# Second mixer matrix of an encoder trunk: three of seven partial sums read out by ScalarE and added on GpSimd

## The chip, the cores and the metric

One Trainium2 chip, one of its cores. The metric is the device time of one execution in microseconds (us); lower is better. A core has TensorE (PE; its weight loads are listed apart as PEld), VectorE (DVE), ScalarE (ACT), GpSimd (POOL) and SyncE (SP), which here issues the DMAs. Each works through its own queue of instructions in the order in which they stand there, and waits on semaphores for the others.

## The reference

Two layers over 1024 tokens of width 1024, all in float32. Each layer mixes tokens with two kinds of attention and then runs a channel mixer with a hidden width of 4096:

```python
h = rmsnorm(x, g_mlp[l]) * (1.0 + scale_m[:, None]) + shift_m[:, None]
x = x + gate_m[:, None] * (jnp.square(jax.nn.relu(h @ w_ff1[l])) @ w_ff2[l])
```

The change lies in the second product of this mixer, `... @ w_ff2[l]`, and in the sum into `x`.

## The kernel before

Everything is held transposed: a tile `xT` has 128 channels on the partitions and 1024 tokens along them, and `xs` is the list of the eight such tiles of the residual `x`.

A float32 product is made from three products of rounded halves. `split` (lines 200 to 202) writes the rounded high part on ACT (a CAST, L201) and the rest on DVE (L202), and `mm3` (L208, L209, L210) multiplies high by high, high by low and low by high into one PSUM bank. The hidden activations come back from memory in the same way through `load_split` (line 1118): a DMA (L1120), a CAST on ACT (L1121) and a subtraction on DVE (L1122).

The mixer (`mixer`) computes 14 sixteenths of the hidden width with a fast block multiplication: seven products, numbered p = 1 to 7, in place of eight. The second matrix runs in steps: `steps` has 21 of them for each layer, each for one output group q (of four) and up to three blocks k of the hidden width. The four groups begin at different blocks, so that the first step has one block, the second two, and the last steps two, one, three and two; the rest have three. `ff2_step` (line 1313) does one product of one step: three matmuls for each block (L208 to L210, 128x512 columns), and then adds the PSUM bank, times the gate, to its quadrant of `x`, with one DVE instruction (L1323). Below, that is called a read-out.

Products of one step share banks, and this is what makes the read-outs urgent:

```python
ORDER = (1, 5, 6, 3, 7, 2, 4)
CHAIN = {1: "x", 6: "x", 7: "x", 4: "x", 5: "z", 3: "z", 2: "y"}
```

Products 1, 6, 7 and 4 accumulate one on top of the other in one bank `px`; 5 and 3 in a bank `pyz`; 2 has a bank of its own, also called `pyz`. Product 6 may not begin before product 1 has been read out, 7 not before 6 has, 4 not before 7 has, and 3 not before 5 has. The banks of the next step are others.

The quadrants of `x` that the products reach: 1 and 2 the same one, 6 and 3 the same one, 5 and 7 the same one, 4 one alone.

Beside the products, DVE and ACT split the weights of products five ahead (`wq`, in eight buffers, L201 and L202) and the activations `ho` (L1121 and L1122). POOL makes the sums of weights that products 5, 6, 3 and 7 need, four for each step (`weight_operands`, L1131), from raw weights `wr` that SP loads (L1177). The tiles of the first matrix's results, `u`, come from a pool of seven buffers (`unit`, line 1194); the second matrix doesn't use it.

The order of instructions in each queue isn't that of the program: a planner goes through it with a model of the costs of its own and orders each queue by the times at which instructions become ready in that model. So a product's matmuls can stand between those of another product, and the first steps of the second matrix run among the last products of the first.

Of the kernel before, what the change touches and what calls it, by code (L numbers as in the profile page):

```python
# [12 lines left out]
AF = mybir.ActivationFunctionType  # L13
ALU = mybir.AluOpType
# [23 lines left out]
def hybrid_trunk(  # L38
# [6 lines left out]
    V, A, G, T = nc.vector, nc.scalar, nc.gpsimd, nc.tensor  # L45
# [31 lines left out]
    def nm(s):  # L77
        uid[0] += 1
        return f"{s}_{uid[0]}"

    def slab(s, shape=(P, 1024), dt=F32):
        return arena.tile(list(shape), dt, tag="slab", name=nm(s))
# [7 lines left out]
    def bank(s="pb"):  # L90
        return psb.tile([P, CH], F32, tag="pb", name=nm(s))

    def cs(ch):
        return slice(ch * CH, (ch + 1) * CH)
# [35 lines left out]
    for i in range(8):  # L130
        t = slab("xrow")
# [150 lines left out]
    ps = bank("ppos")  # L282
# [51 lines left out]
    for ch in range(2):  # L334
        for k in range(8):
            ps = bank("pyT")
# [824 lines left out]
    def mixer(l, hq, gate_m):  # L1161
# [4 lines left out]
        def chain_bank(c):  # L1166
            if c == "x":
                return bank("px")
            return pool["S"].tile([P, CH], F32, tag="S", name=nm("pyz"))
# [17 lines left out]
        def product(ps, w, ops, first):  # L1187

            mm3(ps, [(w[0][:, k, :], w[1][:, k, :], t[:, 0, :], t[:, 1, :]) for k, t in enumerate(ops)], first,
                skip_group_check=True)  # L1190
# [3 lines left out]
        def unit(s):  # L1194
            return pool["ff"].tile([P, CH], F32, tag="u", name=nm(s), bufs=7)
# [117 lines left out]
        def ff2_step(n, p, w, st):  # L1313
            _, q, ks = steps[n]
            c = CHAIN[p]
            if p in FIRST:
                st[c] = chain_bank(c)
            ps = st[c]
            product(ps, w, [ho[k, p] for k in ks], p in FIRST)
            row, ch = {1: (0, 0), 6: (0, 1), 7: (1, 1), 4: (1, 0), 5: (1, 1), 3: (0, 1), 2: (0, 0)}[p]  # L1320
            nt = q + 4 * row
            x = xs[nt][:, cs(ch)]
            V.scalar_tensor_tensor(x, ps, gate_m[:, nt:nt + 1], x, op0=ALU.mult, op1=ALU.add)  # L1323
            for k in ks:
                left[k, p] = left.get((k, p), 4) - 1
                if not left[k, p]:
                    free[0] += 1
# [7 lines left out]
        for n in range(len(work) + AHEAD):  # L1335
            if n < len(work):
                kind, i, p = work[n]
                ws.append(get_w(i, p) if kind == 1 else get_w2(i, p))
            if n >= AHEAD:
                kind, i, p = work[n - AHEAD]  # L1340
                s = st.setdefault((kind, i), {})
                (ff1_step if kind == 1 else ff2_step)(i, p, ws[n - AHEAD], s)
                if kind == 1:
                    if i == 15:
                        free[0] += 8 if p == ORDER[0] else 4
                    if p == 4 and l + 1 < depth and 1 < i < 14 and i % 2:
                        ada(l + 1, (1, 0, 2, 4, 3, 5)[i // 2 - 1], slab, slab)
                fill()
# [115 lines left out]
```

## Time and profile before

| | us |
|---|---|
| median of 3 runs | 3271.41 |
| range of the runs | 3270.94 to 3275.39 |
| the profiled execution | 3277.75 |
| its span, first to last instruction | 3275.9 |
| second matrix, layer 0 | about 1338 to 1635 |
| second matrix, layer 1 | about 2938 to 3214 |

The rows further down are from the page of the profiled execution and from views of its trace. Busy times add up what the records of an engine cover; a PE record overlaps the next one, so a busy PE isn't a PE at its peak. A wait is listed with the instruction that ended last before the waiting one could start. Times in the trace count from the first instruction.

### The profile page before, as it was taken

The page shows a single profiled execution, that of the slowest core. Times are in us where ns is not written, and L with a number is a line of the kernel's source. Part 1 is how long each engine was busy: PE and PEld are TensorE (multiplying, and loading weights), DVE is VectorE, ACT ScalarE, POOL GpSimd, SP SyncE. Part 2 cuts the span into 40 slices and gives each one's busy share as a digit, 9 for nine tenths or more (in the row PEclk, how much of TensorE's full clock was granted, in tenths as well). Part 3 has the DMA queues.
Part 4 walks back from the last instruction along what each step waited for, and adds up shares of the span by engine and source line. Part 5 has one row for each costly group of instructions (what it writes and reads, how often), then busy time and mean ns, then how long its engine had stood idle before and what let it go on. Part 6 is the DMA issues. An engine that isn't in the chain of part 4 may idle for free.

```text
span 3275.9 us, 43644 instructions
## 1 busy us (share of the span) xinstructions
PE 3070.8 (94%) x15104; PEld 2461.4 (75%) x15104; DVE 2334.4 (71%) x3812; ACT 1252.1 (38%) x2436; POOL 857.5 (26%) x876
## 2 busy tenths in 40 slices
PE   6999999999996989999989999999999799999998
PEld 6878886777775767777778788777778577777777
DVE  8566667667559987888864666676763786678885
ACT  5233336553223322444332233365531333343442
POOL 5110112222232232332252101132222323223320
PEclk9999999999998999999999999999999899999999
DMA  6544334115715864644424443341244144464442
GB/s 250 161 125 109 105 93 125 45 54 178 240 65 178 263 215 154 209 145 143 116 100 115 127 113 107 90 126 36 62 138 151 48 161 145 142 212 134 146 126 93
DMA packets 357430, 437.81 MB, mean 134 GB/s; under 512 B 30492, under 2 KB 236506, under 8 KB 357210
## 3 DMA queue, kind: packets, MB, share of 16 engines
q1 hardware_dynamic: 357210, 435.03, 43.3%
q8 instruction: 119, 1.95, 0.3%
q14 instruction: 101, 0.83, 0.1%
HBM read 305.00 MB, written 112.62 MB: 127 GB/s over the span
## 4 chain that ended last, share of the span: by engine, by line
PE 68%; DVE 14%; DMA 8%; issue 4%; POOL 3%; ACT 2%; SPq 1%; DVEq 0%; ACTq 0%; POOLq 0%
PE pd L208 8%; PE pd L209 8%; PE pd L210 8%; PE smla L787 5%; PE px L208 4%; PE pom L821 4%; PE px L210 4%; PE px L209 4%; DVE wq L202 3%; DMA wada<-in_w_ada_dram 3%; PE pyz L210 3%; PE pTm L806 3%; PE pyz L208 3%; PE pyz L209 3%; DMA ho<-hid_d 2%
## 5 line engine op out<-in xcount | busy, mean ns | idle before, releaser
L208 PE MATMUL pd<-h,wh 128*128 128x512 f32 x768 | 308.5, 402 | 1.5 <-ACT wh L201 1.5
L209 PE MATMUL pd<-h,wh 128*128 128x512 f32 x768 | 301.8, 393 | 0.0
L210 PE MATMUL pd<-h,wh 128*128 128x512 f32 x768 | 301.8, 393 | 0.0
L601 POOL TENSOR_SCALAR pna<-pna,sm 128x384 f32<-128x384 f32 x128 | 81.0, 635 | 615.7 <-DVE sm L600 506.0
L794 POOL TENSOR_SCALAR pmla<-pmla,sm 128x1024 f32<-128x1024 f32 x128 | 145.3, 1135 | 339.4 <-DVE sm L793 259.1
L1131 POOL TENSOR_TENSOR s<-wr 128x512 f32<-128x512 f32 (+3 forms) x74 | 98.3, 1329 | 457.6 <-DMA wr<-in_w_ff_dram 292.9
L514 DVE RECIPROCAL gate<-gate 128x512 f32<-128x512 f32 x64 | 214.2, 3347 | 0.7
L208 PE MATMUL px<-h,wq 128*128 128x512 f32 x512 | 204.3, 403 | 10.1 <-ACT u L1205 10.0
L789 DVE TENSOR_REDUCE sm<-smla 128x1 f32<-128x1024 f32 x128 | 156.6, 1224 | 79.2 <-PE smla L787 64.4
L1122 DVE TENSOR_TENSOR ho<-ho 128x512 fp32r<-128x512 f32 x196 | 161.6, 830 | 67.0 <-ACT ho L1121 66.6
L210 PE MATMUL px<-h,wq 128*128 128x512 f32 x512 | 201.1, 395 | 6.1 <-DVE wq L202 6.1
L209 PE MATMUL px<-h,wq 128*128 128x512 f32 x512 | 202.3, 396 | 0.0
L202 DVE TENSOR_TENSOR wq<-s,wq 128x512 fp32r<-128x512 f32 (+3 forms) x296 | 193.6, 670 | 1.8 <-ACT wq L201 1.8
L208 PE MATMUL px<-ho,wq 128*128 128x512 f32 x448 | 176.0, 395 | 19.4 <-DVE xT L1323 18.0
L1121 ACT CAST ho<-ho 128x512 fp32r<-128x512 f32 x196 | 121.2, 621 | 180.0 <-DMA ho<-hid_d 173.4
L792 ACT ACTIVATE pmla<-smla,sm 128x1024 f32<-128x1024 f32 x128 | 142.9, 1117 | 117.9 <-DVE sm L790 115.0
L201 ACT CAST wq<-s 128x512 fp32r<-128x512 f32 (+3 forms) x296 | 154.5, 541 | 87.0 <-PE px L210 28.8
L210 PE MATMUL pyz<-h,wq 128*128 128x512 f32 x384 | 155.8, 406 | 32.2 <-DVE wq L202 32.2
L787 PE MATMUL smla<-st,st 128*128 128x512 f32 x512 | 171.4, 415 | 6.6 <-DMA st<-st 3.5
L202 DVE TENSOR_TENSOR wq<-wr,wq 128x512 fp32r<-128x512 f32 (+3 forms) x222 | 175.0, 806 | 0.4 <-ACT wq L201 0.4
L209 PE MATMUL px<-ho,wq 128*128 128x512 f32 x448 | 174.9, 390 | 0.0
L210 PE MATMUL px<-ho,wq 128*128 128x512 f32 x448 | 173.3, 390 | 0.0
(277 smaller groups left out, 8133.7 us busy)
## 6 DMA issues: line engine op xcount, KB each, us to landing
ho<-hid_d SPq DMA_DIRECT2D x196, 256.0 KB
wada<-in_w_ada_dram SPq DMA_DIRECT2D x96, 512.0 KB
wr<-in_w_ff_dram SPq DMA_DIRECT2D x64, 512.0 KB
w<-in_w_in_dram SPq DMA_DIRECT2D x56, 512.0 KB
hid_d<-u SPq DMA_DIRECT2D x96, 256.0 KB
wr<-in_w_ff_dram SPq DMA_DIRECT2D x64, 384.0 KB
hid_d<-t SPq DMA_DIRECT2D x84, 256.0 KB
gate_d<-gate SPq DMA_DIRECT2D x64, 256.0 KB
```

The costliest lines, as they stand in the source:

```text
L201: pin(A.copy(dst_hi, src))
L202: V.tensor_tensor(dst_lo, src, dst_hi.bitcast(F32), op=ALU.subtract)
L208: T.matmul(ps, wh, mh, start=first and i == 0, stop=False, **kw)
L209: T.matmul(ps, wh, ml, start=False, stop=False, **kw)
L210: T.matmul(ps, wl, mh, start=False, stop=i == n - 1, **kw)
L514: V.reciprocal(g, g)
L787: T.matmul(ps[:, cs(ch)], a[:, t], b[:, cs(ch)], start=i == 0, stop=i == 2)
L789: V.reduce_max(sm[:, 0:1], ps, axis=AX.X)
L792: A.activation(pt, ps, AF.Exp, bias=sm[:, 1:2], scale=MLA_SCALE, accum_out=sm[:, 2:3])
L794: G.tensor_scalar(pt, pt, sm[:, 3:4], 1.0, op0=ALU.mult, op1=ALU.mult)
L821: T.matmul(p[64 * hd:64 * hd + 64, :256], vm[kk][:, h * 64:(h + 1) * 64], pTs[pair, q2, hd][:, kk, :], start=kk == 0, stop=kk == 7)
L1122: V.tensor_tensor(t[:, 1, :], t[:, 1, :].bitcast(F32), t[:, 0, :].bitcast(F32), op=ALU.subtract)
```

## The change

For products 1, 6 and 7 the read-out is now two instructions: ACT copies the bank, times the gate, into a tile `t` from the pool of the `u` tiles, and POOL adds `t` to `x`. Products 5, 3, 2 and 4 are read out by DVE as before.

```diff
             x = xs[nt][:, cs(ch)]
-            V.scalar_tensor_tensor(x, ps, gate_m[:, nt:nt + 1], x, op0=ALU.mult, op1=ALU.add)
+            if p in (1, 6, 7):
+
+                t = unit("part")
+                A.activation(t, ps, AF.Copy, scale=gate_m[:, nt:nt + 1])
+                G.tensor_tensor(x, x, t, op=ALU.add)
+            else:
+                V.scalar_tensor_tensor(x, ps, gate_m[:, nt:nt + 1], x, op0=ALU.mult, op1=ALU.add)
```

## Rows read from the trace of the kernel before

**Rows 1.** The page: busy us (share of the span) xinstructions, and the chain.

```profile
PE 3070.8 (94%) x15104; PEld 2461.4 (75%) x15104; DVE 2334.4 (71%) x3812; ACT 1252.1 (38%) x2436; POOL 857.5 (26%) x876
PE 68%; DVE 14%; DMA 8%; issue 4%; POOL 3%; ACT 2%; SPq 1%; DVEq 0%; ACTq 0%; POOLq 0%
```

**Rows 2.** Busy time by stretch: length, PE, PEld, DVE, ACT, POOL, clock, DMA.

```profile
1338.00:1635.00 297.00, 284.64 (x1228) 229.72 (x1227) 254.19 (x405) 126.90 (x257) 92.36 (x78) 0.99 0.48 146
2938.00:3214.00 276.00, 263.93 (x1147) 214.30 (x1148) 238.78 (x372) 113.14 (x224) 84.44 (x74) 1.00 0.45 138
```

**Rows 3.** Line L1323, whole run: ns min/median/max, and who waited (us, times).

```profile
L1323 DVE SCALAR_TENSOR_TENSOR xT<-px,mod,xT x168: 732/739/753, 1341.0 to 3213.6; 128x512 f32<-128x512 f32 x168
L1323 DVE SCALAR_TENSOR_TENSOR xT<-pyz,mod,xT x126: 729/739/751, 1341.7 to 3209.7; 128x512 f32<-128x512 f32 x126
...
  PE px L208: 18.0, 15
...
  PE pyz L208: 3.5, 2
```

**Rows 4.** Instructions in order of time, 3060 to 3068: start us, us, engine, line.

```profile
3060.79 0.39 PE L208 MATMUL px<-ho,wq 128*128 128x512 f32 x1
...
3062.83 0.39 PE L208 MATMUL pyz<-ho,wq 128*128 128x512 f32 x1
...
3064.49 1.01 POOL L1131 TENSOR_TENSOR s<-wr 128x384 f32<-128x384 f32 x1 [11.39 <-DMA wr<-in_w_ff_dram]
...
3065.09 0.62 ACT L1121 CAST ho<-ho 128x512 fp32r<-128x512 f32 x1 [1.64 <-PE pyz L210]
...
3065.74 1.39 DVE L1122 TENSOR_TENSOR ho<-ho 128x512 fp32r<-128x512 f32 x1 [1.56 <-ACT ho L1121]
...
3065.77 0.39 PE L209 MATMUL px<-ho,wq 128*128 128x512 f32 x1
...
3067.06 0.74 DVE L1323 SCALAR_TENSOR_TENSOR xT<-px,mod,xT 128x512 f32<-128x512 f32 x1
...
3067.85 0.50 PE L208 MATMUL px<-ho,wq 128*128 128x512 f32 x1 [1.69 <-DVE xT L1323]
```

**Rows 5.** Groups of ACT, whole run, by shape: xcount | busy, mean ns | idle.

```profile
L1205 ACT COPY u<-px 128x512 f32<-128x512 f32 x96 | 56.0, 586 | 287.1 <-PE px L210 283.5 <-DVE u L1230 2.2 <-DVE t L1251 1.2
L1041 ACT ACTIVATE xT<-xT,mod,amlp 128x512 f32<-128x512 f32 x16 | 12.4, 807 | 10.9 <-DVE xT L1036 10.9
```

**Rows 6.** Groups of POOL, whole run, by shape.

```profile
L1131 POOL TENSOR_TENSOR s<-wr 128x512 f32<-128x512 f32 x32 | 54.0, 1686 | 108.7 <-DVE wq L202 65.7 <-DMA hid_d<-t 23.5 <-DVE xT L1036 7.3
L241 POOL TENSOR_TENSOR sums<-sums,sq 128x512 f32<-128x512 f32 x30 | 42.3, 1410 | 156.0 <-ACT sq L240 125.6 <-DVE var L248 30.0
```

**Rows 7.** Groups from 2938 to 3214, by shape.

```profile
L1122 DVE TENSOR_TENSOR ho<-ho 128x512 fp32r<-128x512 f32 x83 | 69.9, 846 | 26.7 <-ACT ho L1121 26.7
L1121 ACT CAST ho<-ho 128x512 fp32r<-128x512 f32 x79 | 49.0, 621 | 80.1 <-DMA ho<-hid_d 76.5 <-PE pyz L210 1.6 <-PE px L210 1.1
L202 DVE TENSOR_TENSOR wq<-s,wq 128x384 fp32r<-128x384 f32 x64 | 43.3, 681 | 0.0
L1131 POOL TENSOR_TENSOR s<-wr 128x384 f32<-128x384 f32 x15 | 17.1, 1138 | 132.9 <-DMA wr<-in_w_ff_dram 108.3 <-DVE wq L202 18.2 <-DVE ho L1122 6.5
```

**Rows 8.** Lines L1122 and L202 from 2930 to 3214: ns min/median/max.

```profile
L1122 DVE TENSOR_TENSOR ho<-ho x88: 672/683/1505, 2929.6 to 3168.2; 128x512 fp32r<-128x512 f32 x88
...
L202 DVE TENSOR_TENSOR wq<-s,wq x80: 279/546/1376, 2931.8 to 3200.6; 128x384 fp32r<-128x384 f32 x64, 128x256 fp32r<-128x256 f32 x12, 128x128 fp32r<-128x128 f32 x4
```

**Rows 9.** Start of the second matrix in layer 1, in order of time.

```profile
2944.45 0.68 DVE L1208 SCALAR_TENSOR_TENSOR u<-u 128x512 f32<-128x512 f32 x1
2945.15 0.34 SPq L1211 DMA_DIRECT2D hid_d<-u  x1
```

**Rows 10.** Chain that ended last, 2930 to 3216, in order of time: start us, us, what.

```profile
2999.69 5.43 DMA ho<-hid_d
...
3059.05 5.97 DMA ho<-hid_d
```

## The prediction

> **What bounds the kernel now.** The page comes first: PE is busy for 94% of the span and makes up 68% of the chain that ended last, DVE only 14% [rows 1]. So PE's matmuls set the time, and the change touches none of them. What it can win is time in which PE stands still in the second matrix, and nothing else. The busy times by stretch come next. In both stretches of the second matrix the second-busiest engine is DVE, 254 of 297 us and 239 of 276 us, some 86%, while ACT has 42% and POOL 31% [rows 2]. Hence the third view, the line of the read-outs itself and who waited for it: over the whole run PE stood still for 18.0 us, in 15 places, before a `px` matmul, and 3.5 us, in 2 places, before a `pyz` matmul, because a DVE read-out came late [rows 3]. A `px` product that waits for a read-out waits for that of product 1, 6 or 7: product 4 is the last in its bank, and the next step takes another bank. All 18.0 us therefore hang on the read-outs that are moved, and the 3.5 us on that of product 5, which stays.
>
> Last, one of these waits in order of time, to see why DVE was late [rows 4]. A product is nine matmuls from 3060.79 to 3062.83, or 2.04 us. Its read-out starts at 3067.06, four microseconds after its end, though it takes 0.74 us. In between DVE waits at the head of its queue for ACT's cast of an activation, which starts at 3065.09, and then subtracts it in 1.39 us, twice the median of 0.68 [rows 8], while POOL, whose first sum began at 3064.49, is in the middle of its sums. PE had gone on with matmuls of other products until 3065.77, and then stands still until the read-out ends: 1.69 us by the trace. So a read-out is late not because DVE has no time for it, but because it stands in a queue behind something that is itself late.
>
> **The change part by part.** There are 21 steps in each of two layers, three moved products in each: 126 read-outs, 63 for each layer.
>
> DVE loses 126 of its 294 read-outs, at 739 ns each [rows 3]: 63 x 0.739 = 46.6 us for each layer, of 239 busy in layer 1. This by itself is worth nothing, as PE and not DVE sets the time.
>
> ACT gains 63 copies out of PSUM. The nearest row is its copy of a `px` bank of the same shape into the same kind of tile, 586 ns; the dearest one of this size takes a scale and a bias from a tile, 807 ns [rows 5]. I take 0.6 us, as the bank and the tile are those of the first row: 63 x 0.6 = 38 us, from 113 to 151 busy of 276 (at 0.81 us, 164). ACT has the room. What is queued behind such a copy on ACT are the casts of weights and of activations; the weights are split five products or more ahead, so a copy that waits for its product holds up nothing that is due. Ahead of it stand casts of activations that wait for their DMA: 76.5 us of such waiting in layer 1 [rows 7]. This is the same root as DVE's lateness, one stage earlier: on DVE a read-out stands behind the wait, the cast and the subtraction, on ACT behind the wait and the cast. In the example, a copy that stood right behind the cast of 3065.09 would run from 3065.7 to 3066.3, against 3067.80 now; PE's last matmul began at 3065.77 and the next was due at 3066.0, so some 0.3 us of the wait would be left, about a fifth. Not every place is like this, since at the start of the second matrix ACT runs casts without a break and the products are short. I leave one third of the 18.0 us standing: a gain of 12.0 us. The bounds are 18.0 (nothing left) and about 2 (the copies are held up by the same DMAs for nearly as long).
>
> POOL gains 63 additions of 128x512, two inputs and an output in place. The nearest row has the same form, the running sum of squares, at 1410 ns; sums of the same shape under heavier load took up to 1686 [rows 6]. That is 63 x 1.41 = 89 us (106 at the dear end) on top of 84, or 173 to 190 of 276 us in layer 1. POOL holds that on average. Who waits for POOL now: DVE's read-out of product 3 needs the addition of product 6 into the same quadrant, and that of product 2 needs the addition of product 1. The second has four products' time; the first has one, 2.04 us, and needs 0.6 for the copy and 1.41 for the addition, so it comes just in time when POOL is free, and late by up to the four sums of a step, some 4.6 us at 1.14 each [rows 7], when it isn't. Behind product 3's read-out DVE's whole queue waits. But no product waits for the read-out of 3 itself; the next read-out of DVE that PE needs is product 5 of the next step, five products or 10 us later in a full step. So I count this as cover, not as a loss, in full steps; where it is gone is the second rival.
>
> The rest of DVE's work meets POOL more often. A subtraction of activations takes 672 ns at its shortest and 1505 at its longest [rows 8], with a mean of 846; the subtraction of a weight sum has a median of 546 [rows 8], which I take for its length when nothing disturbs it, and a mean of 681 [rows 7]. That is 83 x 0.174 + 64 x 0.135 = 23 us of stretching in layer 1, for 84 us of POOL [rows 2]: 0.27 us for each us of POOL. The 89 us of additions would then cost DVE 24 us, so of the 46.6 us it keeps 22. The read-outs from PSUM themselves don't stretch: 729 to 753 ns over all 294 [rows 3]. As the two `pyz` waits hang on DVE's lateness, I let them grow by half: a loss of 1.8 us, between 0 and, if they quadrupled, 10.
>
> The Trainium skill, SBUF — State Buffer, section "Who interferes with whom", says that VectorE and GpSimd share one pair of ports, that a VectorE instruction with two SBUF inputs contends with a GpSimd instruction that reads SBUF, and that the later one is blocked until the other ends; one with a single SBUF input isn't touched. The traces agree in kind: the read-outs, with one input in PSUM, never stretch, and the longest subtraction is about its shortest plus most of an addition. By its letter each addition could hold DVE up for its full length, in place of the third that I take; that is the third rival.
>
> The tiles of the pool of seven are new to the second matrix. Its first steps run among the last products of the first matrix, whose `u` tiles are still to be squared and stored: one square starts only at 2944.45 and its store is issued at 2945.15 [rows 9], when the second step is already under way. A copy of the second step may have to wait for that store. Bounds: nothing, or two short products, some 4 us, in each layer; I take 1 us for both layers, as the planner can bring the square forward.
>
> Sum: 12.0 - 1.8 - 1.0 = 9.2 us off the profiled execution's 3277.75, or 0.28%. The median of the runs lies 6.3 us below that execution; the same 9.2 us off the median gives 3262.2.
>
> **The rivals.** First, the lateness only changes its engine: ACT's copies stand behind the same activation loads, the waits move from DVE to ACT and 2 to 5 us are left of the gain, which the two losses eat. For it speaks that the chain runs through an activation load of over 5 us just before two of the waits of layer 1 [rows 10]; against it that ACT is idle for over half of the time and its casts keep their length (the activation cast's mean of 621 ns [rows 7] is the 0.62 us of the example [rows 4]), so that the two causes that lie on DVE, the subtraction and its stretching, fall away. Time: 3269 to 3272, no change. This includes the case that the planner orders the queues anew and what is won in one place is lost in another.
>
> Second, and on the other side: POOL's queue becomes the place where read-outs are late. Its additions stand in order among weight sums, and the first sum of a step waits for its weights, 108 us in layer 1 [rows 7], once 11.39 us [rows 4]. An addition behind it makes DVE's read-out of product 3 late by that much, and DVE then holds up the splits and the read-out of product 5. PE's cover is 10 us in a full step but only 3.4 in a step of one block and 6.8 in one of two; it decides when the addition is over 3.4 us late in the five short steps of a layer, or over 10 in a full one. If in each short step PE loses 2.5 us (about half of the four sums), that is 12.5 us for each layer and 25 in all; less the 12.0 of gain, 13 us slower: 3284. For it speaks the tight timing of product 6 and the length of POOL's waits; against it that the planner puts an addition ahead of a sum that isn't ready in its model.
>
> Third, DVE becomes the bound: each addition blocks DVE for its whole 1.41 us, so DVE has 239 - 46.6 + 89 = 281 us in 276 and the stretch grows by 5 us or more in each layer: 3281 or more. The measured third speaks against it.
>
> **How the numbers follow.** Chances: the forecast (6.5 to 20 us faster) 0.50; the first rival, within 6.5 us, 0.27; the second 0.17, the third 0.06. Predicted 3262. A measurement of this kernel can tell about 0.2%, 6.5 us, from no change. The low end, 3250, is all 21.5 us of waits for read-outs gone; the high end, 3282, takes in the first rival, the third at its mildest and the milder half of the second. The chances of faster, same and slower are 0.50, 0.27 and 0.23.
>
> **What would show it.** PE's waits for L1323 before `px` should be gone, and the waits for the new ACT line be about 6 us in all; the copy should take 0.59 to 0.61 us, the addition 1.3 to 1.5; DVE's busy share in the two stretches should fall from 86% to about 79%, POOL's rise to over 60%, and the mean subtraction of activations grow from 0.84 to over 1.0 us. If PE waits for the new copies as much as it did for DVE, the first rival holds; if DVE's read-outs wait for POOL and PE then for `pyz` or for splits, the second; if DVE's busy share rises, the third. The prediction is wrong if the planner's new order costs PE time in places that have nothing to do with the read-outs.

## The result, and the profile after

The changed kernel takes 3323.88 us at the median of four runs (3315.98 to 3324.31), beside 3271.90 for the kernel before: the ratio is 1.0155, with a 95% interval of 1.0142 to 1.0168. Forecast were 3262 us, in a range of 3250 to 3282. The profiled execution took 3323.59 us, its span is 3321.6, 45.7 us over that of before.

All of it lies in the second mixer matrix. The first view shows the busy times of its two stretches, without the first 9 us in layer 0 and the first 19 in layer 1, in the columns of [rows 2]:

```profile
1340.00:1655.00 315.00, 283.87 (x1192) 222.69 (x1190) 257.41 (x325) 154.66 (x303) 182.31 (x140) 0.99 0.43 131
2958.00:3258.00 300.00, 272.95 (x1151) 216.38 (x1150) 244.88 (x308) 146.80 (x286) 178.60 (x139) 0.98 0.42 128
```

POOL's time doubled, as forecast. DVE lost 126 of its 294 read-outs and is busy as long as before in us (245 in layer 1, where [rows 2] has 239). Its share fell to 82%, because the stretch grew. The lengths come from the starts of the last matmuls of the first and of the second matrix, here of layer 1 (count: ns min/median/max, first and last start, and the last starts are those used):

```profile
L210 PE MATMUL px<-h,wq x512: 387/389/793, 964.1 to 2956.7; 128*128 128x512 f32 x171
...
L210 PE MATMUL px<-ho,wq x448: 387/389/628, 1331.8 to 3257.9; 128*128 128x512 f32 x150
```

From 2956.7 to 3257.9 are 301.2 us; the same two starts lie 276.6 apart in the kernel before. Layer 0 gives 304.6 and 278.7. Together that is 50.5 us more. Below, such a length, of layer 1, is called the stretch.

Whom did PE wait for? Waits of the whole run (us in total, times, longest):

```profile
PE pyz L210 <- DVE wq L202: 68.1, 46, 8.4
...
PE pyz L208 <- DVE xT L1329: 15.2, 13, 5.1
...
PE px L208 <- ACT part L1326: 6.6, 8, 1.3
```

The 18.0 us before `px` [rows 3] are down to 6.6 us, now for ACT's copies. The 3.5 us before `pyz` [rows 3] are 15.2. And the wait for L202, the low halves of weights that DVE splits off, is 68.1 us; the same row of the kernel before reads 32.3, nearly all of it outside the second matrix. The row of the kernel before in the whole run, the same in its second matrix of layer 1 (2938 to 3214), and that of the change there (2940 to 3258):

```profile
PE pyz L210 <- DVE wq L202: 32.3, 23, 7.2
```

```profile
PE pyz L210 <- DVE wq L202: 0.2, 1, 0.2
```

```profile
PE pyz L210 <- DVE wq L202: 14.7, 11, 3.6
```

The three differences make 36 us. The rest lies in short gaps: between matmuls, which start 0.227 us apart when nothing holds them up, the gaps of 0.05 to 0.25 us beyond that add up to 16.3 us in the two stretches, against 5.5 in the kernel before. Most of them stand right behind a wait.

The groups of layer 1 show why DVE is late. Shape, count | busy us, mean ns | idle before, from 2958 to 3258:

```profile
L1327 POOL TENSOR_TENSOR xT<-xT,part 128x512 f32<-128x512 f32 x63 | 91.9, 1466 | 43.0 <-ACT part L1326 43.0
L1122 DVE TENSOR_TENSOR ho<-ho 128x512 fp32r<-128x512 f32 x83 | 91.4, 1105 | 34.3 <-ACT ho L1121 34.3
...
L202 DVE TENSOR_TENSOR wq<-s,wq 128x384 fp32r<-128x384 f32 x64 | 54.4, 857 | 3.7 <-ACT wq L201 3.7
...
L202 DVE TENSOR_TENSOR wq<-wr,wq 128x384 fp32r<-128x384 f32 x48 | 34.0, 714 | 0.6 <-ACT wq L201 0.6
```

Against [rows 7] the subtraction of activations went from 846 to 1105 ns, that of weight sums from 681 to 857, at the same counts: 83 x 0.259 + 64 x 0.176 = 33 us more for these two groups alone. The third group, of weights that are no sums, read in the kernel before (2938 to 3214):

```profile
L202 DVE TENSOR_TENSOR wq<-wr,wq 128x384 fp32r<-128x384 f32 x48 | 28.2, 587 | 0.0
```

A stretch in order of time shows where that lands. First DVE's queue, then the PE rows around the wait:

```profile
3137.73 0.54 DVE L202 TENSOR_TENSOR wq<-s,wq 128x384 fp32r<-128x384 f32 x1
3141.69 1.62 DVE L1122 TENSOR_TENSOR ho<-ho 128x512 fp32r<-128x512 f32 x1 [3.42 <-ACT ho L1121]
3143.23 1.38 DVE L202 TENSOR_TENSOR wq<-s,wq 128x384 fp32r<-128x384 f32 x1
3144.53 1.50 DVE L1122 TENSOR_TENSOR ho<-ho 128x512 fp32r<-128x512 f32 x1
3145.95 0.74 DVE L1329 SCALAR_TENSOR_TENSOR xT<-pyz,mod,xT 128x512 f32<-128x512 f32 x1
3146.61 0.71 DVE L202 TENSOR_TENSOR wq<-s,wq 128x384 fp32r<-128x384 f32 x1
3147.25 1.78 DVE L1122 TENSOR_TENSOR ho<-ho 128x512 fp32r<-128x512 f32 x1
3148.95 0.74 DVE L1329 SCALAR_TENSOR_TENSOR xT<-px,mod,xT 128x512 f32<-128x512 f32 x1
3149.61 0.68 DVE L1122 TENSOR_TENSOR ho<-ho 128x512 fp32r<-128x512 f32 x1
3150.21 1.61 DVE L202 TENSOR_TENSOR wq<-s,wq 128x384 fp32r<-128x384 f32 x1
3151.75 0.68 DVE L1122 TENSOR_TENSOR ho<-ho 128x512 fp32r<-128x512 f32 x1
3152.35 0.54 DVE L202 TENSOR_TENSOR wq<-wr,wq 128x384 fp32r<-128x384 f32 x1
```

```profile
3148.94 0.39 PE L209 MATMUL pyz<-ho,wq 128*128 128x512 f32 x1
3152.95 0.50 PE L210 MATMUL pyz<-ho,wq 128*128 128x512 f32 x1 [3.62 <-DVE wq L202]
```

DVE stands idle for 3.4 us until a late activation has been cast, and then has everything at once. Five of its subtractions take 1.4 to 1.8 us where an undisturbed one takes 0.54 or 0.68. The two read-outs from PSUM among them keep their 0.74. PE needs the low half of a weight that stands at the very end of the row and is still for 3.6 us. The same stretch as busy times (before, in and after the burst):

```profile
3130.00:3141.00 11.00, 11.00 (x49) 8.94 (x48) 8.27 (x12) 4.46 (x9) 5.25 (x5) 1.00 0.55 173
3141.50:3153.00 11.50, 7.88 (x36) 6.21 (x34) 11.31 (x12) 8.17 (x17) 8.63 (x7) 1.00 0.27 79
3153.00:3164.00 11.00, 11.00 (x41) 8.89 (x42) 7.88 (x10) 3.86 (x8) 5.21 (x5) 0.84 0.64 186
```

In the burst DVE is busy for 11.3 of 11.5 us, and POOL, with its own sums and the additions, for 8.6. Before and after it DVE is at 72 to 75%. The 82% of the whole stretch is a mean over these. It isn't the only such place: ahead of each of the 21 times that PE waits over 1 us for DVE in the two stretches, DVE is busy for at least 96% of the last 5 us, and for 82 to 100% of the last 10. The last row also shows what a wait costs behind its end: the granted clock is 0.84 of full in it, so for part of these 11 us TensorE ran at the lower of its two levels, 1.2 GHz and not 2.4, and 41 matmuls went through where the 11 us before the burst held 49.

### The profile page after: what moved, and what is told of

It is laid out like the page before. It is cut to its first block, busy times and chain, and to the rows that moved or that the text cites. A ratio compares the mean times of both kernels' runs of the same rounds, so it can differ in the third digit from the quotient of the medians.

```text
span 3321.6 us, 43772 instructions
## 1 busy us (share of the span) xinstructions
PE 3082.9 (93%) x15104; PEld 2458.7 (74%) x15104; DVE 2350.1 (71%) x3686; ACT 1322.7 (40%) x2562; POOL 1047.5 (32%) x1002
## 4 chain that ended last, share of the span: by engine, by line
PE 67%; DVE 16%; DMA 7%; issue 4%; POOL 3%; ACT 3%; SPq 1%; DVEq 0%; ACTq 0%; POOLq 0%
PE pd L208 8%; PE pd L209 8%; PE pd L210 8%; PE smla L787 5%; DVE wq L202 4%; PE pom L821 4%; PE px L208 4%; PE px L210 4%; PE px L209 4%; PE pyz L210 3%; PE pTm L806 3%; PE pyz L208 3%; PE pyz L209 3%; DMA wada<-in_w_ada_dram 2%; DMA ho<-hid_d 2%
## 5 line engine op out<-in xcount | busy, mean ns | idle before, releaser
L1122 DVE TENSOR_TENSOR ho<-ho 128x512 fp32r<-128x512 f32 x196 | 204.8, 1050 | 82.1 <-ACT ho L1121 82.1
L202 DVE TENSOR_TENSOR wq<-s,wq 128x512 fp32r<-128x512 f32 (+3 forms) x296 | 230.8, 798 | 8.3 <-ACT wq L201 8.3
L1327 POOL TENSOR_TENSOR xT<-xT,part 128x512 f32<-128x512 f32 x126 | 185.2, 1476 | 79.6 <-ACT part L1326 79.6
L202 DVE TENSOR_TENSOR wq<-wr,wq 128x512 fp32r<-128x512 f32 (+3 forms) x222 | 193.7, 894 | 0.7 <-ACT wq L201 0.6
L208 PE MATMUL px<-ho,wq 128*128 128x512 f32 x448 | 176.4, 395 | 6.6 <-ACT part L1326 6.6
L209 PE MATMUL px<-ho,wq 128*128 128x512 f32 x448 | 175.7, 392 | 0.0
```

Source lines behind the costliest of these rows:

```text
L202: V.tensor_tensor(dst_lo, src, dst_hi.bitcast(F32), op=ALU.subtract)
L208: T.matmul(ps, wh, mh, start=first and i == 0, stop=False, **kw)
L209: T.matmul(ps, wh, ml, start=False, stop=False, **kw)
L1122: V.tensor_tensor(t[:, 1, :], t[:, 1, :].bitcast(F32), t[:, 0, :].bitcast(F32), op=ALU.subtract)
L1327: G.tensor_tensor(x, x, t, op=ALU.add)
```

## The experiments

All times are medians beside runs of the kernel before on the same chip (3269.8 to 3270.4 us); "ratio" is to those. A stretch is read from the profiled execution, whose time can lie off the median (12 us under it in e10, 11 in e13, 9 in e5, 6 in e3). Unless said otherwise an edit is to the changed kernel, in its read-out of products 1, 6 and 7.

### Without POOL, and with POOL working for nobody

**e1**: DVE adds the copy.

```diff
-                G.tensor_tensor(x, x, t, op=ALU.add)
+                V.tensor_tensor(x, x, t, op=ALU.add)
```

> ACT copies products 1, 6 and 7 out as in the change, but DVE and not POOL adds the copy to x. Ports (POOL's additions stretch DVE's subtractions of two SBUF tiles): about as before or a little faster, 3258 to 3275 us, since px no longer waits for DVE. POOL's queue (weight sums late behind additions): the same. DVE waiting for POOL's addition of product 6: the same. Copies on ACT, or the planner's new order, as the cause: still slow, 3305 to 3325 us.

Measured: 3261.16 us, ratio 0.9976 (0.9963 to 0.9989), stretch 273.4 us.

**e2**: as e1, and POOL does an addition that nobody needs.

```diff
+                V.tensor_tensor(x, x, t, op=ALU.add)
+                G.tensor_tensor(t, t, t, op=ALU.add)
```

> As e1, and POOL does one addition of the same size for each copy, in place on the copy's tile, after DVE has read it, that nobody needs. Ports: slow like the change, 3305 to 3330 us, with the subtraction of activations at a mean of about 1.05 us again. POOL's queue: slow too, 3305 to 3330. DVE waiting for POOL's addition: fast as e1. Order or ACT: as e1.

Measured: 3309.25 us, ratio 1.0120 (1.0105 to 1.0135), stretch 296.0 us.

**e3**: as e2, but POOL only writes.

```diff
+                V.tensor_tensor(x, x, t, op=ALU.add)
+                for _ in range(3):
+                    G.memset(t, 0.0)
```

> As e2, but POOL writes zeros over the copy's tile three times, about 1.4 us in all, and reads nothing. Ports (read side): fast as e1, within 6 us of it, with the subtraction of activations back at about 0.85 us. POOL's queue: slow like e2. DVE waiting for POOL's addition: fast as e1.

Measured: 3263.94 us, ratio 0.9979 (0.9967 to 0.9991), stretch 271.4 us.

The pair e2 and e3 is the cleanest of the study. The planner put their instructions in nearly the same order (14 of 2562 stand elsewhere on ACT, 13 of 3812 on DVE, 30 of 15104 on PE), POOL is busy for nearly as long, and only one of them reads. POOL's own group in e2 and in e3, whole run:

```profile
L1328 POOL TENSOR_TENSOR part<-part 128x512 f32<-128x512 f32 x126 | 169.3, 1347 | 154.6 <-DVE xT L1327 149.9 <-issue 4.6
```

```profile
L1329 POOL MEMSET part<- 128x512 f32 x378 | 191.8, 525 | 100.6 <-DVE xT L1327 89.8 <-issue 4.6
```

And what DVE's two kinds of subtraction took, in e2 and in e3:

```profile
L1122 DVE TENSOR_TENSOR ho<-ho 128x512 fp32r<-128x512 f32 x196 | 182.1, 935 | 32.8 <-ACT ho L1121 32.7
...
L202 DVE TENSOR_TENSOR wq<-s,wq 128x384 fp32r<-128x384 f32 x128 | 129.7, 1021 | 0.0
```

```profile
L1122 DVE TENSOR_TENSOR ho<-ho 128x512 fp32r<-128x512 f32 x196 | 158.4, 813 | 38.9 <-ACT ho L1121 37.9
...
L202 DVE TENSOR_TENSOR wq<-s,wq 128x384 fp32r<-128x384 f32 x128 | 90.1, 710 | 0.5 <-ACT wq L201 0.5
```

169 us of reading additions, which nothing waits for but the next use of a tile, cost 45 us over 192 us of writing. So it is not POOL's queue, nor the copies on ACT: it is that POOL reads SBUF while DVE subtracts one SBUF tile from another. The Trainium skill, SBUF — State Buffer, section "Who interferes with whom", says just this: two SBUF inputs on VectorE contend with a GpSimd instruction that reads SBUF and not with one that only writes, and an instruction with a single SBUF input (outside certain fast modes) doesn't contend. The runs agree, the read-outs included: all 168 that DVE keeps in the change took 729 to 752 ns.

The records of the single instructions say the same. In the two stretches of the change, the 61 subtractions of activations during which POOL ran nothing took 674 to 680 ns; the 104 others had a mean of 1358 and took up to 1789. In e3, the 38 during which POOL only wrote took 672 to 695.

**e10**: the change, but POOL reads nothing.

```diff
-                G.tensor_tensor(x, x, t, op=ALU.add)
+                for r in (t, t, x):
+                    G.memset(r, 0.0)
```

> The change, but POOL writes zeros three times, twice over the copy's tile and once over the quadrant of x, in place of the addition (so those three products and what x held are left out of the sum): nearly the same time on POOL, the same waits of DVE for POOL, no reading. Ports: 3258 to 3275 us, above e3 only by what waiting for POOL's instruction costs. POOL's queue and the waits for it, with ports nothing: 3310 to 3325 us.

Measured: 3271.06 us, ratio 1.0004 (0.9989 to 1.0018), stretch 273.3 us. Here POOL's queue holds instructions of about the same total length (194 us, in the change 185) and DVE is relieved of all 126 read-outs; the loss against the kernel before is gone. The waits of the change it doesn't repeat: none of DVE's read-outs waited for POOL in it, while five did in the change, for 10.9 us. Nor is its order the change's (252 of 2562 instructions stand elsewhere on ACT), so e2 and e3 stay the clean pair. DVE's busy time from 2924 to 3194 is 199 us, 46 less than in the change. The subtraction of activations is at 738 ns:

```profile
2924.00:3194.00 270.00, 262.75 (x1146) 213.97 (x1146) 199.19 (x302) 146.91 (x283) 164.20 (x255) 1.00 0.45 139
...
L1122 DVE TENSOR_TENSOR ho<-ho 128x512 fp32r<-128x512 f32 x196 | 143.8, 738 | 94.5 <-ACT ho L1121 94.1
```

It shows a second thing. In e10 DVE has 63 instructions fewer in a layer than in e1, additions of 0.70 us each and 44 us in all, and the stretch is the same, 273 us. No gain from the relief shows. The median of e10 even lies 9.9 us above that of e1; its profiled execution was the fastest of ten, and what the 9.9 us are, the order or POOL's queue, is open.

### How the loss goes with POOL's reading

**e4**: the change for product 1 alone.

```diff
-            if p in (1, 6, 7):
+            if p in (1,):
```

> The change for product 1 alone (42 copies and additions instead of 126). Ports: about a third of the stretching; the loss follows the time of POOL's additions and some read-outs of px still wait for DVE: 3275 to 3290 us. DVE waiting for POOL's addition of product 6: no loss, 3262 to 3272 us, as the addition of product 1 has four products' time. Order: any.

Measured: 3296.82 us, ratio 1.0078 (1.0060 to 1.0096), stretch 288.4 us, above the expected 3275 to 3290.

**e7**: as e4, with the addition on DVE.

```diff
-            if p in (1, 6, 7):
+            if p in (1,):
...
-                G.tensor_tensor(x, x, t, op=ALU.add)
+                V.tensor_tensor(x, x, t, op=ALU.add)
```

> As e4 (product 1 alone copied by ACT), but DVE does the addition. Ports: the 42 additions of POOL make the whole loss of e4, so this is as before or a little faster, 3262 to 3272 us. The planner's order for a single copied product: as e4, 3290 to 3300 us.

Measured: 3269.52 us, ratio 1.0002 (0.9992 to 1.0011), stretch 275.7 us. A third of the additions thus cost 27 us, over half of the loss, more than the ports alone in proportion would have it. In the two, 1291 of PE's 15104 instructions stand elsewhere too, so the 27 us may not be the collisions' alone. Product 1 has four products' time until its addition is needed, so no wait for POOL can be the cause: none of DVE's read-outs waited for it in e4.

**e8** and **e11**: as e2, with a lighter instruction on POOL, one input or half of the columns.

```diff
-                G.tensor_tensor(t, t, t, op=ALU.add)
+                G.tensor_scalar(t, t, 1.0, 1.0, op0=ALU.mult, op1=ALU.mult)
```

> As e2, but POOL's idle instruction reads the tile once (multiplied by one) where e2 reads it twice. If any POOL instruction that reads SBUF holds the subtractions up: slow, in proportion to its length, 3290 to 3315 us for 0.8 to 1.4 us each. If only two-input ones do: as e1, 3258 to 3266 us.

```diff
-                G.tensor_tensor(t, t, t, op=ALU.add)
+                G.tensor_tensor(t[:, :CH // 2], t[:, :CH // 2], t[:, :CH // 2], op=ALU.add)
```

> As e2 with POOL's idle addition over half of the columns, so about half as long and as many in number. If the loss against e1 goes with POOL's reading time: half of the 48 us of e2, 3280 to 3290 us. If it goes with the number of collisions: as e2, 3303 to 3312. If short collisions are covered by the slack that DVE has: as e1, 3258 to 3270.

Measured: 3275.11 us (ratio 1.0012, 1.0000 to 1.0024) and 3276.39 us (1.0015, 1.0004 to 1.0027), stretches 280.5 and 280.2 us. Both expectations missed: for e8 neither a slow kernel nor one like e1, for e11 less than half. POOL's rows in e8 and e11 (ns min/median/max):

```profile
L1328 POOL TENSOR_SCALAR part<-part x126: 608/864/3541, 1362.0 to 3210.9; 128x512 f32<-128x512 f32 x126
```

```profile
L1328 POOL TENSOR_TENSOR part<-part x126: 603/862/3551, 1357.4 to 3215.3; 128x256 f32<-128x256 f32 x126
```

Two instructions of the same length cost the same, 14 and 15 us over e1, whether they read one tile or two halves. At a median of 0.86 us instead of the 1.35 of e2 (117 us busy in all instead of 169) the loss against e1 falls from 48 to about 15 us: to a third at about two thirds of the time. So it grows faster than POOL's reading time, as it would where slack is used up first; that reason is argued and not shown.

### What the wait for POOL adds, and the planner's order

**e5**: as the change, with product 6 added by DVE and POOL busy all the same.

```diff
-                G.tensor_tensor(x, x, t, op=ALU.add)
+                (V if p == 6 else G).tensor_tensor(x, x, t, op=ALU.add)
+                if p == 6:
+                    G.tensor_tensor(t, t, t, op=ALU.add)
```

> The change, but product 6 is added to x by DVE, and POOL does an addition of the same size on the copy's tile in its place, so POOL has as many additions as in the change and no read-out of product 3 waits for one. Ports alone: about as e2, 3306 to 3315 us. If waiting for POOL's addition of product 6 makes the rest between e2 and the change, then this is as e2; if the rest comes from the order, from longer single collisions or from elsewhere, it is as the change, 3318 to 3326.

**e9**: as the change, with product 3 sent to another quadrant.

```diff
-            row, ch = {1: (0, 0), 6: (0, 1), 7: (1, 1), 4: (1, 0), 5: (1, 1), 3: (0, 1), 2: (0, 0)}[p]
+            row, ch = {1: (0, 0), 6: (0, 1), 7: (1, 1), 4: (1, 0), 5: (1, 1), 3: (1, 0), 2: (0, 0)}[p]
```

> The change, but product 3 is added to the quadrant of product 4, so that DVE's read-out of it doesn't wait for POOL's addition of product 6 (the sums into x are wrong in two quadrants). POOL's additions and their reads stay. If waiting for that addition makes the rest between e2 and the change, 3303 to 3313 us; if not, 3316 to 3326 us. Ports alone for the whole loss: slow in either case.

Measured: 3372.74 us for e5 (ratio 1.0312, 1.0290 to 1.0334) and 3355.25 us for e9 (1.0261, 1.0242 to 1.0279). Both took the wait for product 6's addition away and both became slower than the change, which neither expectation had. The waits say where, e5 first and then e9:

```profile
PE px L208 <- ACT part L1326: 61.8, 28, 3.8
```

```profile
PE px L208 <- ACT part L1326: 31.9, 17, 3.7
```

Without that wait the planner put the queues in another order, and in it ACT's copies stand behind activation casts that wait for their loads (in e9 in layer 1 alone). That order alone isn't slow: e10 has nearly the order of e5 (22 of 2562 instructions stand elsewhere on ACT, 152 of 15104 on PE) and takes 3271 us. With POOL's reads, and with the 42 additions of product 6 that e5 has on DVE and e10 leaves out, it takes 102 us more. So e5 and e9 don't tell what the wait for POOL is worth, and the 14.6 us between e2 and the change (11 by their ratios) stay unexplained: DVE waits 10.9 us for POOL's additions in the change, its longest subtraction is 1.79 us against 1.53 in e2, and no run here separates the two.

**e6**: as e1, with product 5 copied by ACT too.

```diff
-            if p in (1, 6, 7):
+            if p in (1, 5, 6, 7):
...
-                G.tensor_tensor(x, x, t, op=ALU.add)
+                V.tensor_tensor(x, x, t, op=ALU.add)
```

> As e1, with product 5 copied out by ACT and added by DVE too, so that every read-out that a product waits for is a copy on ACT. If PE's remaining waits before pyz products come from late DVE read-outs: 3254 to 3262 us, a little under e1. If ACT's queue is no better a place than DVE's, or the third DVE addition with two SBUF inputs collides with POOL's sums more often: 3262 to 3272.

Measured: 3311.03 us, ratio 1.0131 (1.0111 to 1.0150), stretch 295.5 us, and no addition of POOL in it; both expectations ended at 3272 or below. PE's waits for the copies:

```profile
PE px L208 <- ACT part L1326: 33.2, 16, 3.8
```

That is the first rival of the prediction at work, though not in the change: copies queued on ACT behind activation casts. In e1 this wait is 4.9 us, so it makes 28 of the 50 us between the two. A fourth copied product was enough for an order in which it happens.

### The lead of the weights

The three share an edit: **e12** is e1 with it, **e13** the change with it, and **e14** the kernel before with it.

```diff
-        AHEAD = 5
+        AHEAD = 6
```

> As e1, with the weights asked for six products ahead and not five, in search of a version better than both. If the waits for DVE's split of weights that are left in e1 come from being asked for late: 3250 to 3258 us. If DVE's place in the queue decides and not the lead, or the eight weight buffers do: as e1 or worse, 3258 to 3290.

> The change, with the weights asked for six products ahead and not five. If PE stands still because DVE's late splits of weights are asked for with too little lead, the second matrix loses at most 10 us for each layer against e12, and the time is 3240 to 3262 us. If DVE falls behind in bursts for as long as the collisions last, whatever the lead: 45 to 55 us over e12, 3285 to 3300 us.

> The kernel before with the weights asked for six products ahead. If e12's gain over e1 is that of the lead alone: 20 us under before, 3245 to 3253 us, nearly all of it in the first matrix. If it needs the copies on ACT: 3262 to 3272 us.

Measured: e12 3240.02 us, ratio 0.9899 (0.9880 to 0.9919); e13 3309.36 us, 1.0109 (1.0089 to 1.0129); e14 3248.95 us, 0.9935 (0.9910 to 0.9960). Stretches 271.4, 303.7 and 273.3 us. The longer lead is worth 21 us to e1 and to the kernel before, and 15 to the change; e12 lies below both of its expectations. Most of it comes in the first matrix: in e12 the second one begins at 2900.7 in layer 1, against 2925.3 in e1, and is only 2 us shorter. It doesn't help the second matrix of the change: e13 is 69 us over e12, more than expected of either theory, and its stretch is no shorter than the 301 us of the change. So one more product of lead in the program doesn't bring the late splits forward. This fits a DVE that falls behind in its bursts whatever the lead; how far ahead the splits then stand in DVE's queue isn't shown. e12 is faster than both kernels, by 1.0% than the one before; e14 against e12 gives 9 us of that to the copies on ACT, hardly more than the two intervals leave open.

## Why the prediction was wrong

**The bound, and the waits to be won: right.** The 18.0 us before `px` were to fall to about 6; they are 6.6. In e1, where the copies stand alone without POOL, the kernel is 8.8 us faster than its own runs of before; the forecast for the whole change was 9.2. That the two numbers are so close is in part luck: e1 wins more before `px` (4.9 us are left) and loses part of it again, as PE's waits for split weights (L202) are 9 us longer in its whole run than in the kernel before.

**The relief of DVE: right, as far as is known, that it is worth nothing by itself.** e10 and e1 are 44 us of DVE's work apart in a layer, with stretches of one length and the lesser work in the slower kernel.

**The stretching of the subtractions: the step that failed, twice.** First its size. From 84 us of POOL and 23 us of stretching in two groups I took 0.27 us for each us of POOL ("the third", further on) and so 24 us for the additions in a layer. The same two groups stretched by 33 us more, 0.36 for each us of the 92 of additions: the rate isn't constant, it was higher with more of POOL's time filled. The third group, which the sum left out, adds 48 x 0.127 = 6, so 39 in all. Second, and more, what it was charged with. I set the stretching off against the 46.6 us of read-outs ("of the 46.6 us it keeps 22"), though a paragraph before I had called that relief worth nothing, and left only a growth of the `pyz` waits by half, 1.8 us. These waits grew by 11.7 us. And the wait for split weights, which grew by 36 us and is the largest part of the loss, has no term in the sum at all: the weights were called five products ahead and therefore covered. In the burst above PE takes a weight 0.1 us after DVE has finished it. A lead in the program's loop is not a lead in the planner's queue, and in e13 one more product of it doesn't shorten the stretch.

**The busy share was the wrong measure.** DVE's 86% was read as room, and the third rival (collisions make DVE the bound, 0.06) was tied to the point where its work exceeds the stretch, 281 of 276 us. The mechanism was this one, but it decides much earlier: DVE works in bursts, 11.5 us long in the windows above, and is at 98% there. Every us of stretching in a burst is a us that PE may have to wait. A full DVE alone doesn't make PE wait, though. The kernel before has such stretches too, and PE goes on at full pace in this one:

```profile
3008.00:3020.00 12.00, 12.00 (x53) 9.92 (x54) 12.00 (x21) 4.69 (x10) 2.48 (x3) 1.00 0.37 109
```

In these 12 us DVE finishes 21 instructions, in the 11.5 us of the burst in the change 12. What counts is what stands in the queue ahead of the split that PE needs, and how long it takes. The price in the rival, 3281 us, was a lower bound, and the range ended at 3282 beside it.

**The second rival, POOL's queue, is refuted as the main cause:** e3 has the queue without the loss, and e2 has most of the loss though nothing but the next use of a tile waits for POOL. How much the wait for product 6's addition adds to the change is open. The sign that the prediction gave for this rival, DVE waiting for POOL and PE then for `pyz` or for splits, did appear in the change, but it doesn't tell the rival from stretched subtractions, which make PE wait in the same places. **The first rival** doesn't hold in the change, but its mechanism is real, as e6 shows.

**Sizes.** ACT's copy took 687 ns and not 0.6 us, above the 0.59 to 0.61 named as a sign and below the dear 0.81:

```profile
L1326 ACT ACTIVATE part<-px,mod x126: 677/687/693, 1351.0 to 3255.9; 128x512 f32<-128x512 f32 x126
```

POOL's addition took 1382 ns at the median, as forecast. What the tiles of the pool of seven cost was forecast at 1 us; no run shows it. At the start of the second matrix of layer 1 the change has one longer wait of 5.1 us that the prediction did not foresee, before a `pyz` matmul at 2970.9. It has the same look as the burst above: from 2957.7 DVE goes through stretched subtractions without a break (three of activations from 2961.06 on take 4.87 us) while POOL has four sums and four additions to do, and the read-out that PE needs stands behind them at 2970.13.

## What to carry to other kernels

Before work goes to POOL, ask what it reads and what DVE does at the time: an instruction that reads SBUF on POOL lengthens DVE's two-input instructions, even if nobody waits for its result, while writes on POOL lengthened nothing here, and DVE's read-outs with one input in PSUM weren't lengthened. Judge the cover of a queue by what it has to do in the ten microseconds ahead of the wait, not by its share over the stage, and don't offset work that is moved away from an engine against delays that fall into its bursts. Where a planner orders the queues, compare variants whose order is the same (e2 with e3); small edits that changed the order moved the time by some 50 us here (e5 beside the change, e6 beside e1), and how much of that the order makes isn't shown.

## What the runs showed of the hardware

A copy out of PSUM on ACT that takes its scale from a tile took 0.1 us longer than a plain one of the same shape: 687 ns at the median against a mean of 586 [rows 5]. POOL's collisions work both ways: in the two stretches of the change the 11 additions that met no two-input instruction of DVE took 1288 to 1293 ns, the 115 others up to 2793, with a mean of 1494. Two POOL instructions of one length, one reading a whole tile once and the other half a tile twice, disturbed DVE to the same extent (e8, e11).
